# Token-wise projections, the residual's carry on another engine, q's rms inside the exponential, and a new order of weights in the last passes

## The chip, the cores and the metric

One core of a Trainium2 chip. The metric is the device time of one execution in microseconds (us); the median of three runs is given. Engines: PE (matrix products), ACT, DVE (vector) and POOL, each with an instruction stream of its own that runs in program order; SP issues the loads.

## The reference

Two layers run over 512 latent and 128 context tokens with 1024 features. Layer 0 mixes tokens by a Hyena long convolution, layer 1 by attention; each layer then has a gated ConvFFN with 2816 hidden features. Cut to what the change touches:

```
z = h @ w_qkv + b_qkv                    # 1024 -> 8 q heads, 2 k heads, 2 v heads of 128
q = z_q * rsqrt(mean(z_q^2) + eps) * q_gain ;  k likewise, with k_gain
q, k = rotate(q), rotate(k)              # rotary positions, latent tokens only
p = softmax(q @ k^T * 128**-0.5) ;  out = (p @ v) @ w_o + b_o
x = layer_norm(alpha * x + (1 + gate) * out) * ln_g + ln_b
h = x * (1 + scale) + shift              # what the next projection reads
```

Latent queries see 512 latent and 256 cached keys, context queries the 128 context keys.

## The kernel before

Everything is float32, and a product of float32 numbers is made of three matmuls over a high and a low half of both operands (`mm3`, L339 to L341): high by high, high by low, low by high. PE therefore reads every weight as a pair of tiles (`whl`): ACT casts the loaded piece to its high half (L334), and DVE or POOL subtracts to get the low half (L335). Loads land in `raw` (three buffers, issued by SP at L226); the pairs rotate through a ring of three, so a cast waits until PE has done with the pair three back.

The 640 tokens are five tiles of 128: `LAT3` = 0, 1, 2, `REST` = 3, 4 (4 is the context), `ALL5`. A projection whose result has tokens on the partitions is a `TokenPass`. `run` goes over the weight pieces j and for each over the tiles, all tiles adding up in PSUM at once; only the last `tail` pieces go tile by tile, and after each tile `done(i)` reads its sums. `hooks` are functions called at a piece's number, which puts their instructions at that place in each engine's stream. `prep` splits the weights, `ahead` pieces before they are used.

**Out-projections** (`out_passes`, `out_projection`): a pass over LAT3, then one over REST with the same weights (the ConvFFN's second half; its first half is an ALL5 pass). When REST starts, three groups of weights are still in the ring, and two groups (`Keep`) stand split in tiles of the old h. Other groups are loaded again. `begin` sets the order of the groups: the ring's oldest, the first kept, the ring's others, the other kept one, then the reloaded ones. After a tile's sums `last` runs on DVE: gate and residual (L634, L639), statistics (L528, L529), a reciprocal root by Newton steps (L511 to L520), then ACT normalises (L542). During REST the hooks `finish` call `make_h` for tiles 0, 1, 2: PE transposes x (L496) and ACT and DVE scale it into the next h. `at` says at which piece: 0, 1, 3 in the Hyena and attention projections, 1, 5, 10 in the ConvFFN's. Tiles 3 and 4 get theirs during the next projection.

**Attention** (`attention`): four passes make k, v (`ps[0]` LAT3, `ps[1]` REST) and q (`ps[2]`, `ps[3]`, four heads each, ALL5), without a tail: all five tiles end together. `biased` adds the bias (L1106), `squares` sums squares on ACT (L1126), `rms` makes the reciprocal roots, `normed` multiplies by them (L1141) and rotates (a product on POOL at L1147, two operations on DVE, L1151 and L1152). `kv_turn` and `q_turn` transpose on PE (L1157). The second half of q (`ps[3]`) is normed and turned inside the attention. There 32 units of work (8 heads by 4 tiles of latent queries) follow one another: scores, maximum (L1277), exponential (L1279), division by the sum on POOL (`normalise`, L1226), transposes (L1286), split, product with v. `carry` multiplies x by alpha times ln_g and adds ln_b's part, ten operations of 128x1024 (L663) over the five tiles, for the residual after the attention; it is on POOL, one operation every second unit from unit 12.

Of the kernel before, what the change touches and what calls it, by code (L numbers as in the profile page):

```python
# [202 lines left out]
class TokenPass:  # L203
# [89 lines left out]
class Build:  # L293
# [320 lines left out]
    def out_passes(self, acts, kt, w, h, tail=3, lag=2):  # L614
# [10 lines left out]
    def out_projection(self, passes, xs, gates, finish, hooks=None, final=None, early=None, mid=None, after=None):  # L625
# [25 lines left out]
        at = (0, 1, 3) if whole else (1, 5, 10)  # L651
# [396 lines left out]
    def qkv_pass(self, h, c, toks, before=None):  # L1048
# [6 lines left out]
        return self.tm_pass(act, KD, self.io["qkv"][c], 1, toks, self.nc.vector, before)  # L1055

    def attention(self, h, hstack, ap, oT, outs, pending, first, carry):
# [9 lines left out]
        st = ExitStack()  # L1067
        rp = self.pool(st, "rope")
# [6 lines left out]
        def prepare():  # L1075
# [7 lines left out]
            for t, j in ((g, 0), (gs, 1)):  # L1083
                nc.sync.dma_start(out=t.rearrange("p a d -> p (a d)"), in_=io["gains"][j:j + 1].broadcast_to([P, 2 * P]))
            for t, nm in enumerate(("k", "q")):
# [17 lines left out]
        def biased(c0):  # L1103
# [24 lines left out]
        def rms(c0, nh, toks, have=()):  # L1128
            n = nh * len(toks)
            for i in toks:  # L1130
                if i not in have:
                    squares(c0, nh, toks, i)
# [352 lines left out]
```

## Time and profile before

| | |
|---|---|
| median of 3 runs | 1657.54 us (1654.52 to 1657.75) |
| profiled execution | 1658.16 us, of which the span is 1656.4 us |
| PE busy | 95% of the span |
| DVE, ACT, POOL busy | 58%, 39%, 31% |
| mean granted TensorE clock | 0.983 |

The profile is of one execution. A row of the timeline gives the start in the span, the time, engine, line, operation and tiles, then in brackets how long the engine had waited and for what. PE works throughout except for the first tenth of the span and a few short stops, so what a change is worth is read at these stops, and at the clock that is granted after them.

### The profile page before, as it was taken

How to read it: one execution, taken by the hardware profiler on the slowest of the kernel's cores; microseconds unless marked ns; L12 is line 12 of the kernel's file. 1: busy time of each engine (PE TensorE's matmuls, PEld its weight loads, DVE VectorE, ACT ScalarE, POOL GpSimd, SP SyncE). 2: the span in 40 equal slices, each digit the busy share in tenths (PEclk: the TensorE clock that was granted, in tenths of full speed). 3: DMA queues.
4: the chain of work that ended last, by engine and by line, in shares of the span. 5: the costliest groups of instructions: out<-in, count | busy, mean ns of one | idle time of the engine just before them, and what ended most of it. 6: DMA issues, size and time to landing. Idle time of an engine off the chain costs nothing.

```text
span 1656.4 us, 23775 instructions
## 1 busy us (share of the span) xinstructions
PE 1580.9 (95%) x9545; PEld 1419.3 (86%) x9545; DVE 959.3 (58%) x1575; ACT 652.8 (39%) x1237; POOL 506.2 (31%) x330
## 2 busy tenths in 40 slices
PE   6799999999999999999999998699999999999996
PEld 3689999978999999998887777698999999997885
DVE  5637467677433443355577668777654365345586
ACT  3433223335433333343445337573543333334331
POOL 4533233400344445430001015720065455430000
PEclk9899999999999999999999999799999999999998
DMA  7776341342344444431234200402212122221231
GB/s 267 252 277 249 136 185 64 135 155 102 128 179 141 165 165 155 152 103 64 80 127 150 70 1 27 165 29 77 102 52 103 52 101 90 102 77 64 76 128 51
DMA packets 35445, 198.66 MB, mean 120 GB/s; under 512 B 3946, under 2 KB 5254, under 8 KB 15494
## 3 DMA queue, kind: packets, MB, share of 16 engines
q1 hardware_dynamic: 35334, 197.13, 33.5%
q8 instruction: 75, 1.23, 0.3%
q14 instruction: 36, 0.29, 0.1%
HBM read 188.91 MB, written 8.20 MB: 119 GB/s over the span
## 4 chain that ended last, share of the span: by engine, by line
PE 82%; DVE 8%; POOL 3%; issue 3%; ACT 3%; DMA 1%; SPq 0%; POOLq 0%; DVEq 0%; ACTq 0%
PE p L339 25%; PE p L341 25%; PE p L340 25%; PE p L398 2%; POOL x L663 1%; DMA raw<-in_w_mod 1%; PE p L496 1%; DVE whl L335 1%; DVE x L639 1%; PE p L1286 1%; DVE small L634 1%; DVE bnst L528 1%; POOL whl L335 1%; ACT act L1126 0%; DVE small L1151 0%
## 5 line engine op out<-in xcount | busy, mean ns | idle before, releaser
L335 POOL TENSOR_TENSOR whl<-raw,whl 128x1024 fp32r<-128x1024 f32 x104 | 255.4, 2460 | 351.1 <-ACT whl L334 291.9
L339 PE MATMUL p<-hhA,whl 128*128 128x384 f32 x880 | 301.4, 342 | 0.0
L341 PE MATMUL p<-hhA,whl 128*128 128x384 f32 x880 | 296.5, 337 | 0.5 <-POOL whl L335 0.5
L340 PE MATMUL p<-hlA,whl 128*128 128x384 f32 x880 | 296.5, 337 | 0.0
L334 ACT CAST whl<-raw 128x1024 fp32r<-128x1024 f32 x193 | 202.3, 1050 | 212.6 <-PE p L340 173.9
L340 PE MATMUL p<-hlB,whl 128*128 128x256 f32 x880 | 247.3, 281 | 0.0
L341 PE MATMUL p<-hhB,whl 128*128 128x256 f32 x880 | 246.9, 281 | 0.0
L339 PE MATMUL p<-hhB,whl 128*128 128x256 f32 x880 | 246.7, 280 | 0.0
L339 PEld LDWEIGHTS p<-hhA,whl 128*128 128x128 f32 x880 | 166.0, 189 | 17.7 <-issue 15.9
L593 ACT ACTIVATE zs<-p,fv 128x128 f32<-128x128 f32 (+1 forms) x264 | 105.0, 435 | 162.5 <-PE p L341 156.7
L341 PEld LDWEIGHTS p<-hhA,whl 128*128 128x128 f32 x880 | 165.8, 188 | 1.4 <-POOL whl L335 1.4
L340 PEld LDWEIGHTS p<-hlA,whl 128*128 128x128 f32 x880 | 165.9, 189 | 0.9 <-issue 0.8
L598 DVE SCALAR_TENSOR_TENSOR act<-zs,fv,act 128x642 f32<-128x642 f32 x44 | 45.5, 1034 | 209.0 <-POOL act L597 209.0
L339 PEld LDWEIGHTS p<-hhB,whl 128*128 128x128 f32 x880 | 166.2, 189 | 0.0
L340 PEld LDWEIGHTS p<-hlB,whl 128*128 128x128 f32 x880 | 165.8, 188 | 0.0
L341 PEld LDWEIGHTS p<-hhB,whl 128*128 128x128 f32 x880 | 165.7, 188 | 0.0
L340 PE MATMUL p<-whl,act 128*128 128x512 f32 x364 | 143.9, 395 | 0.0
L341 PE MATMUL p<-whl,act 128*128 128x512 f32 x364 | 142.1, 396 | 1.6 <-DVE act L335 1.6
L339 PE MATMUL p<-whl,act 128*128 128x512 f32 x364 | 143.3, 394 | 0.0
L335 DVE TENSOR_TENSOR whl<-raw,whl 128x1024 fp32r<-128x1024 f32 x89 | 108.8, 1223 | 47.9 <-ACT whl L334 45.7
L598 DVE SCALAR_TENSOR_TENSOR small<-zs,fv,small 128x642 f32<-128x642 f32 x44 | 41.2, 935 | 128.4 <-POOL small L597 128.4
L597 POOL TENSOR_SCALAR small<-zs,fv 128x642 f32<-128x642 f32 x44 | 46.6, 1059 | 208.0 <-ACT zs L593 208.0
(351 smaller groups left out, 3094.0 us busy)
## 6 DMA issues: line engine op xcount, KB each, us to landing
raw<-in_w_mod SPq DMA_DIRECT2D x48, 1024.0 KB, 5.2
raw<-in_ff_in SPq DMA_DIRECT2D x44, 1024.0 KB, 4.8
raw<-in_ff_out SPq DMA_DIRECT2D x26, 1024.0 KB, 5.0
raw<-in_hy_in SPq DMA_DIRECT2D x12, 1024.0 KB, 6.4
raw<-in_qkv SPq DMA_DIRECT2D x7, 1024.0 KB, 5.1
raw<-in_hy_out SPq DMA_DIRECT2D x6, 1024.0 KB, 7.1
raw<-in_at_o SPq DMA_DIRECT2D x6, 1024.0 KB, 5.0
Kd<-act SPq DMA_DIRECT2D x20, 256.0 KB, 2.9
```

What stands on the lines that cost most here:

```text
L334: self.nc.scalar.copy(out=hi, in_=full)
L335: (lo_eng or self.nc.vector).tensor_tensor(out=lo, in0=full, in1=hi.bitcast(F32), op=ALU.subtract)
L339: mm(out, lhsT=sh, rhs=mh, start=start, stop=False)
L340: mm(out, lhsT=sh, rhs=ml, start=False, stop=False)
L341: mm(out, lhsT=sl, rhs=mh, start=False, stop=stop)
L398: nc.tensor.matmul(ps[32 * j:32 * j + 32, :], lhsT=self.condT[:, k, :], rhs=raw[:, j * 512:(j + 1) * 512], start=(k == 0), stop=(k == KD - 1),
L496: nc.tensor.transpose(out=ps[:, kk * P:(kk + 1) * P], in_=x[:, k * P:(k + 1) * P], identity=self.ident)
L528: nc.vector.bn_stats(out=st[:, j, :], in_=x[:, j * 512:(j + 1) * 512])
L593: nc.scalar.activation(dst, src, AF.Identity, bias=bias)
L597: nc.gpsimd.tensor_scalar(out=t, in0=zs[:, 1:1 + WO], scalar1=w[1], scalar2=cb, op0=ALU.mult, op1=ALU.add)
L598: nc.vector.scalar_tensor_tensor(out=t, in0=zs[:, 0:WO], scalar=w[0], in1=t, op0=ALU.mult, op1=ALU.add)
L634: nc.vector.tensor_tensor(out=t, in0=p, in1=g[:, cs], op=ALU.mult)
```

## The change

**Out-projections.** The REST pass takes the ring's three groups first, then the reloaded ones, then the two kept. Its tail grows from 3 to 5 pieces of 8 in the Hyena and attention projections and from 4 to 8 (layer 0) or 10 (layer 1) of 22 in the ConvFFN. New hooks `t0`, `t1`, ... run ahead of each tile of the tail, and the pass that follows gets two of its pieces prepared before the tail. The places of `finish` become 2, `t0`, `t1` (Hyena), 1, 4, 9 (ConvFFN) and 0, 1, `t0` (attention).

**qkv passes.** All four get a tail of 4 pieces of 8. The squares follow each tile's bias at once, and in the q passes the norm of the tile before. Tables, cache loads, norms and turns of k move to other hooks. The second half of q is normed at the end of `ps[3]` and turned at units 1, 3, 5, 7, 9.

**q's rms in the exponential.** q is no longer multiplied by its reciprocal root (ten operations of L1141 go). The root times 128**-0.5 is a number per query: its negative multiplies the row's maximum, and it is the exponential's scale, a column instead of a constant.

**The carry** goes from POOL to DVE, from the attention to hooks of `ps[2]` and `ps[3]`, with row buffers of its own.

Cut to its core, the diff:

```diff
@@ TokenPass.begin
-        held = p.ring[:1] + (p.keep.groups[:1] if p.keep else []) + p.ring[1:] + (p.keep.groups[1:] if p.keep else [])
-        self.ws = {g: p.ws[g] for g in held}
-        gs = held + [g for g in range((self.kt + self.wk - 1) // self.wk) if g not in held]
+        kept = p.keep.groups if p.keep else []
+        self.ws = {g: p.ws[g] for g in p.ring + kept}
+        gs = p.ring + [g for g in range((self.kt + self.wk - 1) // self.wk) if g not in self.ws] + kept
@@ TokenPass.run
         self.prep(kt - 1)
+        if follow:
+            follow.prep(1)
...
-        for i in self.toks:
+        for t, i in enumerate(self.toks):
+            for f in hooks.get(f"t{t}", ()):
+                f()
             for j in range(kt - self.tail, kt):
                 product(j, i)
             done(i, [outs[i, n] for n in range(nn)])
@@ out_passes (end=8, for the ConvFFN of layer l: 8 + 2 * l)
-            return p + [self.tm_pass(act, kt, w, 2, REST, v, p[0], tail=3, ahead=2)]
+            return p + [self.tm_pass(act, kt, w, 2, REST, v, p[0], tail=5, ahead=2)]
...
-        return p + [self.tm_pass(act, kt, w[1], 1, REST, v, p[1], tail=4, ahead=4)]
+        return p + [self.tm_pass(act, kt, w[1], 1, REST, v, p[1], tail=end, ahead=4)]
@@ out_projection (Hyena: at=(2, "t0", "t1"), attention: at=(0, 1, "t0"))
-        at = (0, 1, 3) if whole else (1, 5, 10)
+        at = at or (1, 4, 9)
@@ qkv_pass
-        return self.tm_pass(act, KD, self.io["qkv"][c], 1, toks, self.nc.vector, before)
+        return self.tm_pass(act, KD, self.io["qkv"][c], 1, toks, self.nc.vector, before, tail=4)
@@ attention, biased (q_norm now passes None for the root)
                 zb[c0, i] = z
+                squares(c0, nh, toks, i)
+                if nh == 4 and i:
+                    q_norm(c0 // 512, i - 1)
@@ attention, rms
+                nc.vector.tensor_scalar_mul(ng, rs, -SCALE)
+                nc.vector.tensor_scalar_mul(ps, rs, SCALE)
@@ attention, normed
-            nc.vector.tensor_tensor(out=z, in0=z, in1=rs.broadcast_to([P, nh, P]), op=ALU.mult)
+            if rs is not None:
+                nc.vector.tensor_tensor(out=z, in0=z, in1=rs.broadcast_to([P, nh, P]), op=ALU.mult)
@@ attention, the passes
-        ps[0].run(biased(1024), plan((2, pending[0]), (3, prepare), (4, pending[1]), (6, caches)), ps[1])
-        ps[1].run(biased(1024), plan((0, rms, 1024, 2, LAT3), (0, kv_norm, 0), (2, kv_norm, 1), (3, kv_turn, 0), (4, kv_norm, 2),
-                                     (6, kv_turn, 1)), ps[2])
...
+        carry = self.carry(xs, self.dn, nc.vector, lambda s: rp.tile(s, F32, tag="row", name=self.uid("row"), bufs=2), True)
+        ps[0].run(biased(1024, 2, LAT3), plan((1, next, prep), (2, next, prep), (3, pending[0]), ("t0", pending[1]), ("t1", next, prep),
+                                              ("t2", caches)), ps[1])
+        ps[1].run(biased(1024, 2, REST), plan((0, rms, 1024, 2, LAT3), (0, kv_norm, 0), (1, kv_norm, 1), ("t0", kv_turn, 0),
+                                              ("t0", kv_norm, 2), ("t1", kv_turn, 1)), ps[2])
+        ps[2].run(biased(0, 4, ALL5), plan((0, rms, 1024, 2, REST), (0, kv_norm, 3), (1, kv_norm, 4), (1, kv_turn, 2), (2, next, carry),
+                                           (3, next, carry), (3, next, carry), ("t0", kv_turn, 3), ("t0", next, carry), ("t1", kv_turn, 4),
+                                           ("t1", next, carry)), ps[3])
+        ps[3].run(biased(512, 4, ALL5), plan((0, bias, 512), (0, q_norm, 0, 4), (0, rms, 0, 4, ALL5), *[(i, q_turn, 0, i) for i in range(4)],
+                                             *[(i, next, carry) for i in range(4)], ("t0", next, carry), ("t0", q_turn, 0, 4),
+                                             *[(f"t{u + 2}", first_scores, u) for u in range(2)]))
...
+        q_norm(1, 4)
@@ attention, scores
-                nc.vector.tensor_scalar_mul(mx, mx, -SCALE)
-                nc.scalar.activation(pr, s[:, :, 0:384], AF.Exp, bias=mx, scale=SCALE, accum_out=sm)
+                ng, sc = row_scales(u)
+                nc.vector.tensor_tensor(out=mx, in0=mx, in1=ng, op=ALU.mult)
+                nc.scalar.activation(pr, s[:, :, 0:384], AF.Exp, bias=mx, scale=sc, accum_out=sm)
...
-                if u >= 12 and u % 2 == 0:
-                    next(carry, None)
```

The tables below are the compiled order of instructions: line, operation, output<-inputs, shape. In the changed file lines stand 5 to 23 further down (L335 is L340, L496 is L501, L663 is L668, L1106 is L1114, L1141 is L1160, L1147 is L1166, L1157 is L1176).

The first place is PE at the start of the Hyena projection's REST pass (xyr is the split input, x_826 is tile 0's x). Before:

```order
L339 MATMUL p_433_3267<-whl_3503,hhA_3442 128x512
L340 MATMUL p_433_3267<-whl_3504,hhA_3442 128x512
L341 MATMUL p_433_3267<-whl_3503,hlA_3443 128x512
L496 MATMUL p_496_3649<-ident,x_826 128x128 x4
L496 MATMUL p_498_3661<-ident,x_826 128x128 x4
L339 MATMUL p_492_3645<-whl_3314,xyr_3476 128x512
L340 MATMUL p_492_3645<-whl_3315,xyr_3476 128x512
```
Now:

```order
L345 MATMUL p_494_3647<-whl_3343,xyr_3511 128x512
L346 MATMUL p_494_3647<-whl_3342,xyr_3511 128x512
L344 MATMUL p_495_3648<-whl_3342,xyr_3511 128x512
L345 MATMUL p_495_3648<-whl_3343,xyr_3511 128x512
L346 MATMUL p_495_3648<-whl_3342,xyr_3511 128x512
L501 MATMUL p_501_3683<-ident,x_826 128x128 x4
L501 MATMUL p_503_3695<-ident,x_826 128x128 x4
L344 MATMUL p_492_3645<-whl_3503,xyr_3511 128x512
```
The transposes of tile 0 stood ahead of the pass's first product; now 24 products of it (1985 to 2008 in PE's stream) go first.

The second place is the end of `ps[1]`. On PE before (hhB and hlB are h of REST, small_8355 and small_8357 are k of tiles 0 and 1):

```order
L341 MATMUL p_1063_8362<-whl_8316,hlB_6968 128x512
L339 MATMUL p_1062_8361<-whl_8316,hhB_6967 128x512
L340 MATMUL p_1062_8361<-whl_8317,hhB_6967 128x512
L341 MATMUL p_1062_8361<-whl_8316,hlB_6968 128x512
L1157 MATMUL p_1073_8420<-ident,small_8355 128x128 x2
L339 MATMUL p_1063_8362<-whl_8316,hhB_6967 128x512
L340 MATMUL p_1063_8362<-whl_8317,hhB_6967 128x512
L341 MATMUL p_1063_8362<-whl_8316,hlB_6968 128x512
L1157 MATMUL p_1078_8456<-ident,small_8357 128x128 x2
L339 MATMUL p_1062_8361<-whl_8446,hhB_6967 128x512
```
Now (small_8319 and small_8341 are k of tiles 0 and 1; hhA with p_1087 is `ps[2]`):

```order
L344 MATMUL p_1067_8372<-whl_8428,hhB_6967 128x512
L345 MATMUL p_1067_8372<-whl_8429,hhB_6967 128x512
L346 MATMUL p_1067_8372<-whl_8428,hlB_6968 128x512
L1176 MATMUL p_1079_8438<-ident,small_8319 128x128 x2
L1176 MATMUL p_1084_8468<-ident,small_8341 128x128 x2
L344 MATMUL p_1087_8490<-whl_8434,hhA_6965 128x512
L345 MATMUL p_1087_8490<-whl_8435,hhA_6965 128x512
```
The transposes stood in the middle of the pass's 48 products; now they are behind all of them and ahead of `ps[2]`.

On DVE at the same place, before:

```order
L335 TENSOR_TENSOR whl_8447<-raw_8444,whl_8446 128x1024
L518 TENSOR_TENSOR sd_1070_8376<-rq_1068_8374 128x6
L519 TENSOR_TENSOR sd_1070_8376<-sd_1070_8376,ve_1069_8375 128x6
L520 SCALAR_TENSOR_TENSOR rq_1068_8374<-sd_1070_8376,rq_1068_8374 128x6
L1141 TENSOR_TENSOR small_8355<-small_8355,rq_1068_8374 128x256
L1141 TENSOR_TENSOR small_8357<-small_8357,rq_1068_8374 128x256
L1141 TENSOR_TENSOR small_8359<-small_8359,rq_1068_8374 128x256
L1151 TENSOR_TENSOR small_8355<-small_8355,kta 128x256
L1151 TENSOR_TENSOR small_8357<-small_8357,kta 128x256
L1152 TENSOR_TENSOR small_8355<-small_8355,act_8391 128x256
L1152 TENSOR_TENSOR small_8357<-small_8357,act_8410 128x256
L1151 TENSOR_TENSOR small_8359<-small_8359,kta 128x256
```
Now:

```order
L340 TENSOR_TENSOR whl_8533<-raw_8432,whl_8532 128x1024
L523 TENSOR_TENSOR sd_1070_8376<-rq_1068_8374 128x6
L1114 TENSOR_TENSOR small_8485<-p_1067_8372,qkvb_8212 128x512
L524 TENSOR_TENSOR sd_1070_8376<-sd_1070_8376,ve_1069_8375 128x6
L340 TENSOR_TENSOR vl<-small_8462,vh 128x256
L525 SCALAR_TENSOR_TENSOR rq_1068_8374<-sd_1070_8376,rq_1068_8374 128x6
L340 TENSOR_TENSOR whl_8582<-raw_8579,whl_8581 128x1024
L1160 TENSOR_TENSOR small_8319<-small_8319,rq_1068_8374 128x256
L1160 TENSOR_TENSOR small_8341<-small_8341,rq_1068_8374 128x256
L1160 TENSOR_TENSOR small_8366<-small_8366,rq_1068_8374 128x256
L1170 TENSOR_TENSOR small_8319<-small_8319,kta 128x256
L1170 TENSOR_TENSOR small_8341<-small_8341,kta 128x256
```
k's norm stood ahead of the bias additions of `ps[1]` (L1106); now both bias additions (L1114), that of tile 4 among them, and the split of the pair whl_8581, whl_8582 stand ahead of the norm (L1160, L1170).

The third place is POOL inside the attention, before:

```order
L663 TENSOR_TENSOR x_828<-x_828,raw_9545 128x1024
L663 TENSOR_TENSOR x_829<-x_829,raw_9545 128x1024
L1226 TENSOR_SCALAR raw_9329<-raw_9329,sm_9384 128x2x384
L663 TENSOR_TENSOR x_3261<-x_3261,raw_9545 128x1024
L663 TENSOR_TENSOR x_826<-x_826,raw_9985 128x1024
L663 TENSOR_TENSOR x_827<-x_827,raw_9985 128x1024
L663 TENSOR_TENSOR x_828<-x_828,raw_9985 128x1024
L663 TENSOR_TENSOR x_829<-x_829,raw_9985 128x1024
L1226 TENSOR_SCALAR pr_9435<-pr_9435,sm_9437 128x768
L1147 TENSOR_TENSOR qkvb_9538<-small_8967,qtb 128x512
```
Now:

```order
L1249 TENSOR_SCALAR raw_8922<-raw_8922,sm_1166_8967 128x2x384
L1166 TENSOR_TENSOR qkvb_9001<-small_8953,qtb 128x512
L1166 TENSOR_TENSOR qkvb_9024<-small_8994,qtb 128x512
L1249 TENSOR_SCALAR raw_9047<-raw_9047,sm_9049 128x2x384
L1249 TENSOR_SCALAR raw_9047<-raw_9047,sm_9077 128x2x384
L1249 TENSOR_SCALAR raw_9112<-raw_9112,sm_9114 128x2x384
L1249 TENSOR_SCALAR raw_9112<-raw_9112,sm_9162 128x2x384
```
The operations on x are gone from between the divisions by the sum. On DVE, whose hooks for them stand in `ps[2]` and `ps[3]`, the compiled order has all ten between the transposed tile 3 in `ps[0]` and the first turn of k behind `ps[1]`.

## Rows read from the trace of the kernel before

**Rows 1.** The page, part 1: busy time, share of the span, instructions.
```profile
PE 1580.9 (95%) x9545; PEld 1419.3 (86%) x9545; DVE 959.3 (58%) x1575; ACT 652.8 (39%) x1237; POOL 506.2 (31%) x330
```

**Rows 2.** Timeline of PE: start, us, engine, line, operation, tiles, [wait before it].
```profile
368.80 0.40 PE L339 MATMUL p<-whl,hhA 128*128 128x512 f32 x1
...
369.27 0.40 PE L341 MATMUL p<-whl,hlA 128*128 128x512 f32 x1
374.32 1.82 PE L496 MATMUL p<-ident,x 128*128 128x128 f32 x8 [4.65 <-ACT x L542]
...
927.88 0.44 PE L1157 MATMUL p<-ident,small 128*128 128x128 f32 x2 [1.53 <-DVE small L1152]
...
975.33 1.11 PE L1157 MATMUL p<-ident,small 128*128 128x128 f32 x4 [3.19 <-DVE small L1152]
```

**Rows 3.** Busy time by stretch, as headed; PEclk is the granted clock.
```profile
core 0: us, PE busy (x) PEld busy (x) DVE busy (x) ACT busy (x) POOL busy (x), PEclk, DMA share, GB/s
374.50:377.90 3.40, 3.40 (x13) 3.02 (x13) 3.40 (x16) 1.87 (x4) 0.00 (x0) 0.50 0.02 5
975.30:978.70 3.40, 3.37 (x12) 3.00 (x13) 3.40 (x5) 1.17 (x2) 1.48 (x1) 0.50 0.02 5
1038.60:1043.50 4.90, 4.90 (x22) 4.80 (x23) 3.81 (x8) 1.36 (x3) 4.90 (x3) 0.50 0.00 0
1055.00:1060.60 5.60, 5.56 (x26) 5.56 (x27) 4.34 (x5) 2.61 (x6) 4.88 (x3) 0.50 0.72 227
```

**Rows 4.** PE's waits from 890 to 1120: us in total, times, longest.
```profile
PE p L1286 <- POOL pr L1226: 9.7, 4, 8.1
PE p L1157 <- DVE small L1152: 6.3, 3, 3.2
PE p L339 <- DVE pl L335: 4.8, 2, 4.5
PE p L496 <- ACT x L542: 2.0, 2, 1.2
PE s L339 <- ACT raw L1279: 1.4, 1, 1.4
```

**Rows 5.** Timeline of POOL from 1025 to 1060: carry operations in one piece.
```profile
1042.04 12.06 POOL L663 TENSOR_TENSOR x<-x,raw 128x1024 f32<-128x1024 f32 x5
```

**Rows 6.** Timeline of ACT: make_h's predecessor at 373, a weight cast at 931.
```profile
373.03 1.24 ACT L542 ACTIVATE x<-x,nm,rs 128x1024 f32<-128x1024 f32 x1 [6.62 <-DVE nm L539]
...
931.85 1.05 ACT L334 CAST whl<-raw 128x1024 fp32r<-128x1024 f32 x1 [1.70 <-PE p L340]
```

**Rows 7.** Timeline of DVE around k's norm, 922 to 935.
```profile
924.11 1.64 DVE L1141 TENSOR_TENSOR small<-small,rq 128x256 f32<-128x256 f32 x3
...
931.69 1.28 DVE L1106 TENSOR_TENSOR small<-p,qkvb 128x512 f32<-128x512 f32 x2
932.93 1.23 DVE L335 TENSOR_TENSOR whl<-raw,whl 128x1024 fp32r<-128x1024 f32 x1
```

**Rows 8.** By line: number, ns min/median/max, first and last start.
```profile
L663 DVE TENSOR_TENSOR x<-x,raw x20: 1212/1220/3428, 604.1 to 1390.4; 128x1024 f32<-128x1024 f32 x20
...
L1151 DVE TENSOR_TENSOR small<-small,qta x8: 678/1218/2850, 971.2 to 1056.3; 128x512 f32<-128x512 f32 x8
...
L1147 POOL TENSOR_TENSOR qkvb<-small,qtb x4: 1259/1274/1292, 1019.2 to 1055.0; 128x512 f32<-128x512 f32 x4
```

**Rows 9.** The end: last matmul on PE, then DVE.
```profile
1642.77 0.40 PE L341 MATMUL p<-whl,hid_r 128*128 128x512 f32 x1
...
1644.47 0.68 DVE L634 TENSOR_TENSOR small<-p,bc 128x512 f32<-128x512 f32 x1
...
1648.47 1.41 DVE L1445 SCALAR_TENSOR_TENSOR x<-x,rs,lnb 128x512 f32<-128x512 f32 x2
```

**Rows 10.** The page, part 6: KB, us from issue to landing; then SP's timeline.
```profile
raw<-in_hy_out SPq DMA_DIRECT2D x6, 1024.0 KB, 7.1
...
356.99 0.33 SPq L226 DMA_DIRECT2D raw<-in_hy_out  x1
```

More of the change, by code (lines that the diff above doesn't have):

```diff
@@ L612, in act_split, with out_passes @@
         return act, lambda k: full.rest(self, k)
-    def out_passes(self, acts, kt, w, h, tail=3, lag=2):
+    def out_passes(self, acts, kt, w, h, tail=3, lag=2, end=8):
         v = self.nc.vector
@@ L1054, in act, with attention @@
             return [r]
-        return self.tm_pass(act, KD, self.io["qkv"][c], 1, toks, self.nc.vector, before)
-    def attention(self, h, hstack, ap, oT, outs, pending, first, carry):
+        return self.tm_pass(act, KD, self.io["qkv"][c], 1, toks, self.nc.vector, before, tail=4)
+    def attention(self, h, hstack, ap, oT, outs, pending, first, xs):
         nc, io, tc = self.nc, self.io, self.tc
@@ L1126, in squares, with rms @@
                 nc.scalar.activation(sq[:, j], zb[c0, i][:, j], AF.Square, accum_out=sums[c0][:, t * nh + j:t * nh + j + 1])
-        def rms(c0, nh, toks, have=()):
+        def rms(c0, nh, toks):
             n = nh * len(toks)
-            for i in toks:
-                if i not in have:
-                    squares(c0, nh, toks, i)
             ss = sums.pop(c0)
@@ L1136, in rms @@
             self.rstd(ss, rs.rearrange("p h o -> p (h o)"), n, 1)
+            if nh == 4:
+                ng = rp2.tile([P, n], F32, name=f"ng{c0}")
+                ps = rp2.tile([P, n], F32, name=f"ps{c0}")
+                rs = rs.rearrange("p h o -> p (h o)")
+                nc.vector.tensor_scalar_mul(ng, rs, -SCALE)
+                nc.vector.tensor_scalar_mul(ps, rs, SCALE)
+                for t, i in enumerate(toks):
+                    scales[c0, i] = ng[:, t * nh:(t + 1) * nh], ps[:, t * nh:(t + 1) * nh]
+                return
             for t, i in enumerate(toks):
@@ L1229, in attention @@
         ps = [first, self.qkv_pass(h, 2, REST, first)] + [self.qkv_pass(h, c, ALL5) for c in (0, 1)]
-        ps[0].run(biased(1024), plan((2, pending[0]), (3, prepare), (4, pending[1]), (6, caches)), ps[1])
-        ps[1].run(biased(1024), plan((0, rms, 1024, 2, LAT3), (0, kv_norm, 0), (2, kv_norm, 1), (3, kv_turn, 0), (4, kv_norm, 2),
-                                     (6, kv_turn, 1)), ps[2])
-        ps[2].run(biased(0), plan((0, rms, 1024, 2, REST), (0, kv_norm, 3), (1, kv_norm, 4), (2, kv_turn, 2), (4, kv_turn, 3),
-                                  (5, kv_turn, 4)), ps[3])
-        ps[3].run(biased(512), plan((0, bias, 512), (0, rms, 0, 4, ALL5), *[(i, q_norm, 0, i) for i in range(5)],
-                                    *[(i + 2, q_turn, 0, i) for i in range(5)], *[(6, first_scores, u) for u in range(2)]))
+        prep = prepare()
+        carry = self.carry(xs, self.dn, nc.vector, lambda s: rp.tile(s, F32, tag="row", name=self.uid("row"), bufs=2), True)
[9 more added lines that the diff above has]
+                                             *[(f"t{u + 2}", first_scores, u) for u in range(2)]))
+        for _ in carry:
+            pass
+        q_norm(1, 4)
         hstack.close()
@@ L1404, in run @@
         pending = self.out_projection(passes, xs, lambda: env["gates"], finish, {3: [hook]}, None,
-                                      *[lambda i=i: self.ffn_first(0, i) for i in range(3)])
+                                      *[lambda i=i: self.ffn_first(0, i) for i in range(3)], (2, "t0", "t1"))
         bst.close()
@@ L1414, in run @@
             act = self.act_split(hid)
-            passes = self.out_passes(act, KF, io["ff_out"][l], lambda: env["h"])
+            passes = self.out_passes(act, KF, io["ff_out"][l], lambda: env["h"], end=8 + 2 * l)
             fill = self.mods_units(1, (0, 1, 2)) if l == 0 else iter(())
```

29 lines of the change are left out of this document (17 added, 12 removed).

## The prediction

> **What bounds the kernel now.** I read the page's busy times first: PE is busy for 95% of the span [rows 1], and the change leaves the number of matmuls as it is. So time can come only from PE's stops, from the slower clock behind them, and from what runs after the last matmul. The timeline of PE gives three stops on which the change acts, of 4.65, 1.53 and 3.19 us [rows 2]; the reader is to see the tile that PE waited for. The table by stretch shows what follows a stop: PE is full, yet the granted clock is 0.50, the lower of its two levels (1.2 and 2.4 GHz), for 3.4 us after the stops of 4.65 and 3.19, for 4.9 and 5.6 us after two in the attention [rows 3]. Half of such a stretch is lost, 1.7 to 2.8 us. The waits of PE from 890 to 1120 [rows 4] name the causes there. The largest is 8.1 us for one division on POOL, and POOL's timeline shows why: five carry operations, 12.06 us in one piece, stood ahead of it [rows 5].
>
> **The change part by part.** The sum is made against the profiled execution, 1658.16 us, 0.6 above the median of the runs.
>
> *Hyena's REST pass.* Tile 0's transposes wait for its normalisation on ACT, which ends at 373.03 + 1.24 = 374.27 [rows 6], and start at 374.32 [rows 2]; PE had been idle since 369.67. Now 24 products of the pass stand ahead. Products there start 0.235 us apart (368.80 to 369.27 for two [rows 2]), so they take 5.6 us, and the stop of 4.65 is covered if the normalisation ends no later than before. It may: the projection's last steps run on DVE as they did, and if they slip by half of the stop, 1.3 is left. I take it as covered but for 0.1, and with it go 1.7 of half clock: **-6.3** (bounds -3.3, the 1.3 and its clock left, and -6.4). Tiles 1 and 2 are later by as much as their transposes are.
>
> *Weights in a new order.* Casts and subtractions are as many as before. The reloaded groups are now wanted after the ring's three and not after five. The last load of the Hyena projection is issued at 356.99 and a load takes 7.1 us [rows 10], so it has landed at 364, over 5 us before the pass starts at 369.67: nothing. The same order holds in the other three REST passes; its risk is a rival below.
>
> *ConvFFN of layer 0.* With more of the tail, tiles 3 and 4 end further apart, and their transposes in `ps[0]` come after the normalisation instead of before it. The two waits for L542, 2.0 us [rows 4], go: **-2.0** (0 to -2.0).
>
> *k's first turn.* This is a new wait. The transposes were among the products of `ps[1]`, where they waited 1.53 us [rows 2]. They are now behind the pass's last product, and on DVE k's norm is behind the bias addition of tile 4 and behind the split of a pair whose slot the same last product frees. So nothing of it can begin before PE stops. The cast takes 1.05 on ACT [rows 6], the subtraction 1.23, the bias addition (0.64, half of 1.28) lies beside the cast [rows 7]. From the norm's first product to the transposes were 927.88 - 924.11 = 3.77 us [rows 2, 7]. Together 6.1 us of stop. One or two carry operations, 1.22 each [rows 8], may still be unfinished when PE stops: up to 8.5. I take 7.2 and, between the 1.7 after a stop of 3.19 and the 2.8 after one of 8.1, 2.5 for the clock; the old 1.53 goes: **+8.2** (bounds -1.5, if the scheduler's order costs nothing, and +9.8). Behind the waiting transposes on PE is all of `ps[2]`; nothing on DVE waits for them.
>
> *The carry in `ps[0]` and `ps[1]`.* Ten operations of 1.22 [rows 8] are 12.2 us on DVE in about 30 us where it had gaps. PE sees them where a subtraction for a pair comes late: **+0.3** (0 to +2).
>
> *q's first turn.* It waited 3.19 for a norm that started only after all of q was summed. The multiplication by the root is gone and the rotation runs tile by tile in the tail, ahead of the next pass. The stop goes, and 1.7 of half clock [rows 2, 3]: **-4.9** (0 to -4.9).
>
> *The attention.* Waits on POOL's divisions (9.7), on the split of the probabilities (4.8), on the exponential (1.4) and 1.6 of the turns (6.3 less 1.53 and 3.19) are 17.5 us [rows 4]; the two stretches of 4.9 and 5.6 us at half clock add 5.25 [rows 3]. All of it stood where POOL ran the carry or where the second half of q was normed between units, and both are gone. What is new is at its start: the last rotations of q's second half. Each needs a POOL product of 1.27 and then one on DVE of 0.68 to 2.85 [rows 8], they share one scratch tile, and the maximum of unit 2 stands among them on DVE, its exponential behind them. One round takes 1.95 to 4.1. PE had no slack there, it already waited 1.4 at this place. So 1.4 at least, 1.4 + 2 x 4.1 = 9.6 at most; I take 1.4 + 4.1 = 5.5, one round at its longest or two at their shortest, and 1.7 of clock; and later once more 1.4. New 8.6, old 22.75: **-14.2** (bounds -21.4 and -8.3, with 2.8 of clock).
> The exponential's scale as a column has no row of its own; L542 on ACT has a column for the scale too and takes 1.24 for 1024 elements [rows 6], so I cost it at nothing.
>
> *The end.* The last matmul ends at 1643.17, but tile 4's first step on DVE comes at 1644.47, 1.3 late, and tile 3's last one (1.41 at 1648.47) stands between its steps [rows 9]. With a tail of 10 pieces tile 3 is done long before: **-2.6** (0 to -2.7).
>
> Sum: -6.3 - 2.0 + 8.2 + 0.3 - 4.9 - 14.2 - 2.6 = -21.5, which gives 1636.7; against the median 1636. The forecast is **1636 us**.
>
> **The rivals.** *The new waits are small (1621 us).* If the norm of k is done when PE gets there, 8.2 goes; if unit 2's maximum is no later than before, so do the 7.2 above the 1.4. 1636 - 15.4 = 1621. For it: before, DVE did k's norm in 3.77 us inside a running pass [rows 7]. Against: the order of DVE, where the norm is behind a cast that PE's last product releases.
>
> *DVE becomes the bound (1649 us).* The carry on DVE has 1.22 as its median but 3.43 as its longest, and DVE's rotation has 0.68 and 2.85 [rows 8]: both read two inputs. If the ten carry operations and the rotations of the attention's start are all long ones, DVE is up to 10 x 2.2 = 22 us later between `ps[0]` and the attention; PE sees what is behind it at k's turn and at unit 2's maximum, about half, and the time is 1636 + 13 = 1649. It decides at whether POOL's products run at the same moments. Against it: POOL has only k's and q's rotation there, a few microseconds in all, since the weights of these passes are split by DVE. The Trainium skill, "SBUF — State Buffer", in the section that says who interferes with whom, has DVE and GpSimd share a pair of ports as an exclusive lock, which a DVE operation with two SBUF inputs takes against a GpSimd operation that reads SBUF, the later one being blocked to the end of the earlier one; the page speaks against moving the carry beside POOL's products, and the rotation's longest, 2.85 [rows 8], agrees with it, since it lay beside an operation of the carry on POOL. By it the carry costs this rival's time only where the two streams meet.
>
> *Slower: late weights (1676 us).* The two kept groups gave the reloads time at the head of each of four REST passes. If a reload now lands after the ring's three groups are used up, PE waits up to a load, 7.1 us [rows 10], and runs 2.8 us longer at half clock: 4 x 9.9 = 40 us, 1636 + 40 = 1676. It decides where a load is issued less than 7.1 us and a cast and subtraction (2.3) before its place. Against it: the one place with rows has 12 us from issue to the pass's start.
>
> *It does not do what it says.* The divisions on POOL could be late without the carry too, as 32 of them are still there. Then some 8 of the 14.2 stay: 1644, inside the range.
>
> **How the numbers follow.** Forecast (with 1628 to 1645 as its own range) 0.52; small waits 0.20; DVE as the bound, the unmoved divisions with it, 0.22; late weights 0.06. The second and third case spread to both sides of their time by the bounds of the single costs, so the range goes 2 or 3 us past each, 1619 to 1652; it leaves out some 0.06 of either and all of the last, 0.18. What a measurement here can tell from no change is 0.2%, 3.3 us. A third-case result high enough to be within it has 0.03, late weights in one or two passes only another 0.01. So faster 0.91, same 0.04, slower 0.05.
>
> **What would show it.** In the profile after: no wait for L542 (L547 there) of over 1 us at the Hyena's REST pass, and no half clock behind it; one new wait of 6 to 8.5 us for k's rotation right after `ps[1]`, with about 5 us at 0.50 behind it; no wait of over 1 us at q's turn; no wait for POOL of over 2 us in the attention, one of about 5 near its start; the last matmul followed by less than 8 us on DVE. I am wrong if REST passes wait for weights, if the attention's waits are the same in sum, or if the carry's operations on DVE have a median far above 1.2.

## The result, and the profile after

The changed kernel takes 1632.8 us (median of 4 runs, 1632.59 to 1633.5) against 1657.32 before (4 runs): ratio 0.9859, 95% interval 0.9845 to 0.9874, 24.5 us less. The profiled execution's span is 1631.1 us, with a mean granted clock of 0.988.

The page's busy times, which answer to [rows 1]:

```profile
PE 1574.6 (97%) x9545; PEld 1413.9 (87%) x9545; DVE 961.2 (59%) x1579; ACT 656.5 (40%) x1237; POOL 479.0 (29%) x320
```

PE's busy time fell by only 6.3 us while the span fell by 25.3. So most of what went was time in which PE stood, the end of the span included, and the rest half clock, at which the same products are busy for longer.

PE's waits from 350 on (us in total, times, longest), which answer to [rows 4]:

```profile
PE p L1176 <- DVE small L1171: 7.3, 1, 7.3
PE s L344 <- ACT raw L1312: 4.3, 1, 4.3
PE p L346 <- DVE act L340: 1.6, 2, 0.8
PE p L1319 <- POOL pr L1249: 1.3, 2, 1.0
PE p L1319 <- ACT oT L1203: 1.2, 1, 1.2
PE s L344 <- ACT pr L1312: 1.2, 1, 1.2
```

The waits of [rows 4] on L542 (L547 now) and on POOL's long division are gone; the longest for a division is 1.0. Two large ones are new: 7.3 us for k's rotation and 4.3 us for the exponential of unit 2. PE's timeline has the first right behind the last product of `ps[1]`:

```profile
920.01 0.40 PE L346 MATMUL p<-whl,hlB 128*128 128x512 f32 x1
927.72 1.11 PE L1176 MATMUL p<-ident,small 128*128 128x128 f32 x4 [7.32 <-DVE small L1171]
```

Busy time by stretch, as in [rows 3], shows what the two stops cost beyond themselves. The clock falls to 0.50 while PE stands and stays there for 5.1 and 3.2 us of full work, 2.5 and 1.6 us lost:

```profile
core 0: us, PE busy (x) PEld busy (x) DVE busy (x) ACT busy (x) POOL busy (x), PEclk, DMA share, GB/s
922.60:927.70 5.10, 0.00 (x0) 0.00 (x0) 4.48 (x10) 1.43 (x9) 2.62 (x3) 0.50 0.83 284
927.70:932.80 5.10, 5.08 (x14) 4.16 (x15) 4.93 (x15) 0.75 (x2) 0.00 (x0) 0.50 0.00 0
1001.30:1004.50 3.20, 3.19 (x12) 3.09 (x13) 3.05 (x6) 1.64 (x4) 0.91 (x1) 0.50 0.61 218
```

After the last matmul ([rows 9] before) DVE goes on at once with tile 4, and tile 3's last step (1619.06) is already through. First PE, then DVE:

```profile
1620.18 0.39 PE L346 MATMUL p<-hhB,hid_r 128*128 128x512 f32 x1
```

```profile
1619.06 1.41 DVE L1475 SCALAR_TENSOR_TENSOR x<-x,rs,lnb 128x512 f32<-128x512 f32 x2
1620.60 0.69 DVE L639 TENSOR_TENSOR small<-p,bc 128x512 f32<-128x512 f32 x1
...
1625.98 1.41 DVE L1475 SCALAR_TENSOR_TENSOR x<-x,rs,lnb 128x512 f32<-128x512 f32 x2
```

The table gives the length of each stretch in PE's timeline, in us, from one stage's first product to the next's; the first begins where Hyena's LAT3 pass ends, the last runs from the last matmul to the span's end. All runs of this study are in it. It leaves out what lies ahead of LAT3's end, which differed by up to 6 us between profiled executions (1.0 between before and after), in stages that no run changes. Each row is of one profiled execution.

| run | Hyena REST | ConvFFN 0 | k, v passes | q passes | attention | out-proj., ConvFFN 1 | end | sum |
|---|---|---|---|---|---|---|---|---|
| before | 31.4 | 496.5 | 34.5 | 65.9 | 121.8 | 523.6 | 13.2 | 1286.9 |
| after | 25.1 | 496.4 | 38.5 | 63.0 | 105.8 | 523.3 | 10.5 | 1262.6 |
| control | 25.1 | 496.4 | 38.8 | 63.0 | 105.7 | 523.3 | 10.5 | 1262.7 |
| turns_late | 25.1 | 496.4 | 30.1 | 63.8 | 106.3 | 523.3 | 10.5 | 1255.4 |
| scratch | 25.1 | 496.4 | 38.3 | 63.3 | 102.6 | 523.3 | 10.5 | 1259.6 |
| carry_pool | 25.1 | 496.4 | 32.0 | 61.0 | 124.0 | 522.9 | 10.4 | 1271.8 |
| rest_old | 31.3 | 496.1 | 41.3 | 62.2 | 106.9 | 523.7 | 13.2 | 1274.7 |
| keep_old | 27.7 | 497.9 | 42.7 | 62.4 | 107.0 | 524.5 | 12.5 | 1274.7 |
| tails_old | 27.2 | 496.6 | 40.8 | 63.1 | 105.8 | 523.6 | 13.2 | 1270.3 |
| carry_raw | 25.1 | 496.4 | 32.6 | 62.5 | 107.1 | 523.3 | 10.5 | 1257.4 |
| raw_scratch | 25.1 | 496.4 | 33.6 | 62.3 | 102.1 | 523.3 | 10.5 | 1253.2 |
| q_old | 25.1 | 496.4 | 38.4 | 66.6 | 102.6 | 523.3 | 10.4 | 1262.8 |
| best1 | 25.1 | 496.4 | 29.8 | 61.6 | 102.9 | 523.2 | 10.5 | 1249.4 |
| best1_q_old | 25.1 | 496.4 | 29.9 | 65.0 | 103.3 | 523.3 | 10.4 | 1253.3 |

Between before and after: -6.3 in Hyena's REST pass, +4.0 in the k, v passes, -2.9 in the q passes, -16.0 in the attention, -2.7 at the end.

### The profile page after: what moved, and what is told of

Same layout as the page of the kernel before. It is cut to its first block, busy times and chain, and to the rows that moved or that the text cites. A ratio compares the mean times of both kernels' runs of the same rounds, so it can differ in the third digit from the quotient of the medians.

```text
span 1631.1 us, 23761 instructions
## 1 busy us (share of the span) xinstructions
PE 1574.6 (97%) x9545; PEld 1413.9 (87%) x9545; DVE 961.2 (59%) x1579; ACT 656.5 (40%) x1237; POOL 479.0 (29%) x320
## 4 chain that ended last, share of the span: by engine, by line
PE 85%; DVE 6%; issue 4%; POOL 2%; ACT 2%; DMA 1%; SPq 0%; POOLq 0%; DVEq 0%; ACTq 0%
PE p L344 26%; PE p L345 26%; PE p L346 26%; PE p L403 2%; PE p L1319 1%; DMA raw<-in_w_mod 1%; PE s L344 1%; PE s L346 1%; PE s L345 1%; PE p L501 1%; POOL whl L340 1%; DVE whl L340 1%; DMA row<-dn 0%; DVE x L668 0%; ACT whl L339 0%
## 5 line engine op out<-in xcount | busy, mean ns | idle before, releaser
L340 POOL TENSOR_TENSOR whl<-raw,whl 128x1024 fp32r<-128x1024 f32 x104 | 255.6, 2461 | 347.1 <-ACT whl L339 291.1
L340 DVE TENSOR_TENSOR whl<-raw,whl 128x1024 fp32r<-128x1024 f32 x89 | 108.6, 1222 | 35.9 <-ACT whl L339 33.3
```

What stands on the lines that cost most here:

```text
L340: (lo_eng or self.nc.vector).tensor_tensor(out=lo, in0=full, in1=hi.bitcast(F32), op=ALU.subtract)
```

## The experiments

All are edits of the changed kernel, with ratios to the kernel before on the same chip. The control, the changed kernel again, gave 0.9862 [0.9848, 0.9877].

> The changed kernel itself, unaltered, so that the runs beside it have it on the same chip. All theories: its ratio to the kernel before is again 0.986, the stop at k's turn again 7.3 us.

It held: 1632.96 us, and a stop of 7.3 us.

**turns_late: k's turns inside the first q pass.**

```diff
-    ("t0", kv_turn, 0), ("t0", kv_norm, 2), ("t1", kv_turn, 1)), ps[2])
+    ("t0", kv_norm, 2)), ps[2])
...
-    (1, kv_norm, 4), (1, kv_turn, 2), (2, next, carry),
+    (1, kv_norm, 4), (2, kv_turn, 0), (3, kv_turn, 1), (3, kv_turn, 2), (2, next, carry),
```

> The changed kernel, with k's turns of tiles 0, 1, 2 moved behind the second and third piece of the first q pass (30 and 45 products) instead of right behind the last k, v pass. Theory (the stop of 7.3 us is only a matter of where the transposes stand: k's norm cannot start on DVE before the pass ends): the stop falls to under 0.6 us, the 5 us at half clock behind it (2.5 lost) go too, so 1632.8 - 9.5 = about 1623. Rival (DVE is simply too loaded there, with the carry among its work): the stop comes back at the later transposes or at a weight split of the first q pass, and no more than 3 us are won, 1630 or more.

Measured 1625.37, ratio 0.9823 [0.9807, 0.9839]. The stretches fall by 7.2 us. The theory's direction holds, and the rival's 1630 did not come; the theory asked for 9.5, and 2.0 us of waits stayed at the later turns.

**carry_pool: the carry back on POOL.**

```diff
-    carry = self.carry(xs, self.dn, nc.vector, lambda s: rp.tile(s, F32, tag="row", name=self.uid("row"), bufs=2), True)
+    carry = self.carry(xs, self.dn, nc.gpsimd, self.raw, True)
...
+    if u >= 12 and u % 2 == 0:
+        next(carry, None)
```

> The changed kernel with the carry back on POOL, one operation every second unit from unit 12 of the attention, as before the change; all else as in the change. Theory (the carry on POOL made the long waits of the attention): waits for POOL's divisions and for DVE's splits of about 8 to 12 us in sum come back, with 2 to 5 us at half clock, so 1632.8 + 10 to 14 = about 1645; k's turn waits about 1.2 us less, 6.1 instead of 7.3. Rival (the norms of q's second half between the units made them, and these stay gone): less than 4 us are lost, 1636 or less.

Measured 1640.59, ratio 0.9918 [0.9902, 0.9934]. The attention is 18.3 us longer than in the changed kernel. PE is busy for 106.0 of its 124.0 us, against 97.0 of 105.8, so 9.3 us of this are stops and 8.9 half clock: the carry's place made most of its long waits. The one wait of 8.1 for a division did not come back; the longest is 2.0. But the k, v and q passes are 8.6 shorter, so that the time is under the 1645 expected. PE's waits:

```profile
PE s L344 <- ACT raw L1308: 8.0, 2, 4.4
PE p L1315 <- POOL pr L1249: 4.5, 5, 2.0
PE p L344 <- DVE pl L340: 1.9, 1, 1.9
...
PE p L1176 <- DVE small L1171: 1.6, 1, 1.6
```

k's turn waits 1.6, not the 6.1 I expected. DVE's timeline in this run shows why: the multiplication by k's root (L1160) starts at 912.10, straight behind the last Newton step. The steps from L517 on had begun at 909.06 and took 3.0 us, with one weight split among them:

```profile
911.90 0.17 DVE L525 SCALAR_TENSOR_TENSOR rq<-sd,rq 128x6 f32<-128x6 f32 x1
912.10 1.64 DVE L1160 TENSOR_TENSOR small<-small,rq 128x256 f32<-128x256 f32 x3
```

In the changed kernel the same steps (L517 to L525) begin at 913.61, behind five carry operations (L668). Among them and ahead of the multiplication stand three more carry operations, four weight splits of 1.21 us and two bias additions (L1114). They take 10.2 us, and the multiplication comes at 923.84, behind the pass's end at 920.4:

```profile
913.61 0.16 DVE L517 TENSOR_SCALAR rq<-ve 128x6 int32<-128x6 int32 x1
913.68 1.22 DVE L668 TENSOR_TENSOR x<-x,row 128x1024 f32<-128x1024 f32 x1
914.82 0.15 DVE L523 TENSOR_TENSOR sd<-rq 128x6 f32<-128x6 f32 x1
914.90 1.21 DVE L340 TENSOR_TENSOR whl<-raw,whl 128x1024 fp32r<-128x1024 f32 x1
916.03 0.15 DVE L524 TENSOR_TENSOR sd<-sd,ve 128x6 f32<-128x6 f32 x1
916.11 1.21 DVE L668 TENSOR_TENSOR x<-x,row 128x1024 f32<-128x1024 f32 x1
917.24 0.15 DVE L525 SCALAR_TENSOR_TENSOR rq<-sd,rq 128x6 f32<-128x6 f32 x1
...
919.20 1.21 DVE L668 TENSOR_TENSOR x<-x,row 128x1024 f32<-128x1024 f32 x1
...
920.41 1.21 DVE L340 TENSOR_TENSOR whl<-raw,whl 128x1024 fp32r<-128x1024 f32 x1
...
921.62 0.68 DVE L1114 TENSOR_TENSOR small<-p,qkvb 128x512 f32<-128x512 f32 x1
...
922.71 1.21 DVE L340 TENSOR_TENSOR whl<-raw,whl 128x1024 fp32r<-128x1024 f32 x1
923.84 1.08 DVE L1160 TENSOR_TENSOR small<-small,rq 128x256 f32<-128x256 f32 x3
925.54 1.79 DVE L1170 TENSOR_TENSOR small<-small,kta 128x256 f32<-128x256 f32 x2 [0.62 <-POOL act L1166]
```

So the stop at k's turn seems to be the carry's doing.

**carry_raw: the carry on DVE, later.** This tests that directly.

```diff
-    carry = self.carry(xs, self.dn, nc.vector, lambda s: rp.tile(s, F32, tag="row", name=self.uid("row"), bufs=2), True)
+    carry = self.carry(xs, self.dn, nc.vector, self.raw, True)
```

> The changed kernel with the carry still on DVE, but its rows loaded into the three raw buffers of the weights and not into buffers of their own; a row's load then waits for its turn in that ring, and the second row's five operations come on DVE behind k's norm (10 us later than now). Theory, formed from the run with the carry on POOL, where k's turn waited 1.6 and not 7.3 us: the carry's operations, one between each two steps of k's reciprocal root, push k's norm behind the pass's end; the order of DVE I had put the stop down to is their doing. So the stop falls from 7.3 to under 3 us, with its 2.5 at half clock: 5 to 8 us faster than the control. Rival (the transposes' place behind the pass is enough for the stop): 6 us of it stay, under 2 us faster. A price to look for in both: splits of weights in the q passes that wait for a load, up to 2 us.

Measured 1625.11, ratio 0.9817 [0.9802, 0.9832]. The k, v passes take 32.6 instead of 38.8 and the stop is 2.0; the attention is 1.3 longer than the control's. For the stop the theory holds, and the rival falls. Half clock came all the same: PE runs at 0.50 from 917.4 to 920.8, 1.7 us lost, so most of the 2.5 was not won. turns_late took the stop away with the carry in its old place. So the stop needs both, the transposes right behind the pass and the carry ahead of the norm.

**scratch: a third buffer for q's scratch.**

```diff
-    qb[c0] = rp.tile([P, 512], F32, tag="qkvb", name=f"qkvb{c0}", bufs=2)
+    qb[c0] = rp.tile([P, 512], F32, tag="qkvb", name=f"qkvb{c0}", bufs=3)
...
-    t = rp.tile([P, 512], F32, tag="qkvb", name=self.uid("qkvb"), bufs=2)
+    t = rp.tile([P, 512], F32, tag="qkvb", name=self.uid("qkvb"), bufs=3)
```

> The changed kernel with three instead of two buffers for the bias rows and q's scratch tiles, so that the second half of q has two scratch tiles for its squares and POOL products. Theory (at the start of the attention the maximum of unit 2 is late because POOL's products wait for the one scratch tile): the waits of 4.3 and 1.4 us there shrink by 4 to 6 us and with them most of the 1.6 us lost to half clock, so 1626 to 1629. Rival (the sum of DVE's and ACT's work behind the last q pass is what takes the time, whatever the buffers): under 1 us is won, 1632 or more.

Measured 1630.76, ratio 0.9857 [0.9842, 0.9871], not told apart from the control by the runs. The trace has the attention 3.1 us shorter than the control's: the wait of 4.3 is gone, one of 2.2 for a split is new:

```profile
PE p L1319 <- DVE pl L340: 2.2, 1, 2.2
```

The buffer is one cause and DVE's work behind it the next, so the answer lies between the two theories.

**raw_scratch: both edits.**

> The two edits together: the carry's rows in the raw buffers, and three buffers for q's bias rows and scratch tiles. If the two act at different places, as the theory has it, their gains add up: what the run with the rows in raw buffers wins, and 3 us more (the third buffer took 3.0 us out of the stretch from the end of the last q pass to the attention's out-projection). Rival (they share a cause, DVE's load): clearly less than the sum.

Measured 1623.15, ratio 0.9803 [0.9787, 0.982]. By the stretches 9.6 us won against 5.3 and 3.2 for the edits alone: they add up.

**q_old: q's handling as before.**

```diff
+    nc.vector.tensor_tensor(out=z, in0=z, in1=rs.broadcast_to([P, nh, P]), op=ALU.mult)
...
-    nc.scalar.activation(pr, s[:, :, 0:384], AF.Exp, bias=mx, scale=sc, accum_out=sm)
+    nc.scalar.activation(pr, s[:, :, 0:384], AF.Exp, bias=mx, scale=SCALE, accum_out=sm)
...
+    *[(2 * i + 6, q_norm, 1, i) for i in range(5)], *[(2 * i + 7, q_turn, 1, i) for i in range(5)]
```

> The changed kernel with q's handling as before: q multiplied by its root, first half normed and turned in the second q pass, second half normed and turned between the units of the attention, constant scale in the exponential; the carry stays on DVE. Theory (q's part is worth the stop at q's first turn, 3.19 us and 1.7 at half clock, and inside the attention little either way, since the carry made the long waits there): 4 to 8 us slower than the control, the attention within 3 us of it. Rival (the norms between the units were half of the attention's waits): 12 us or more slower.

Measured 1634.54, ratio 0.9869 [0.9854, 0.9883]. Neither theory held. The stop at q's turn is back (the 10.5 here are 7.3 at k's turn and 3.2 at q's), and the q passes are 3.6 us longer; but the attention is 3.1 shorter. Its start no longer holds the second half's rotations, and the wait for the exponential there is 0.9, not 4.3. In the changed kernel q's part wins nothing that can be told: 0.1 us by the stretches, 1.6 by the medians. The attention also confirms the carry's price: with q's old handling it takes 102.6 us here and 121.8 in the kernel before, with the carry on POOL, 19.2 more, and with the new handling it was 18.3.

```profile
PE p L1164 <- DVE small L1159: 10.5, 2, 7.3
```

**rest_old: the out-projections' part undone.** The old lines of the diff for `begin`, the tails and `at`, of which the first:

```diff
-    gs = p.ring + [g for g in range((self.kt + self.wk - 1) // self.wk) if g not in self.ws] + kept
+    gs = held + [g for g in range((self.kt + self.wk - 1) // self.wk) if g not in held]
```

> The changed kernel with the part on the out-projections undone: order of the weight groups, tails of the REST passes (3, 4, 4) and places of finish as before; the qkv passes and the attention as in the change. Theory (that part is worth the Hyena's stop, 6.2 us with its half clock, and the end, 2.7; the order of the weights by itself nothing): 1632.8 + 8.9 = about 1642, and up to 2.4 more if the waits for tiles 3 and 4 in the first k, v pass come back too, 1644. Rival (the new order of weights takes away waits in every REST pass): 1648 or more.

Measured 1643.93, ratio 0.9934 [0.9917, 0.9952], 12 us slower by the stretches: Hyena's pass +6.2, the k, v passes +2.8, the end +2.7. The theory's upper end.

**keep_old: the order of the weights alone.** The old lines of `begin` only, as in the diff just above.

> The changed kernel with the weight groups of the REST passes in the old order (kept groups early, reloaded last), tails and places of finish as in the change. Theory (the gains of that part come from where the transposes and the tails stand; the order of the weights only moves which products come when, and loads are early in both): the same as the changed kernel within 0.2%, 1630 to 1636, every stretch between the passes' ends within 0.5 us. Rival (the reloads need the new order, or the kept groups' tiles are written by the next h too late in the new one): a stretch of a REST pass changes by 2 us or more.

Measured 1644.57, ratio 0.9931 [0.9918, 0.9945]. My theory fell: with the new tails in the old order all 12 us are lost. From its waits:

```profile
PE p L1176 <- DVE small L1171: 8.1, 1, 8.1
...
PE p L501 <- ACT x L547: 2.8, 2, 2.1
PE p L344 <- ACT hhA L339: 2.5, 1, 2.5
```

The compiled order of PE shows the reason. In the changed kernel the last ConvFFN's tail is 18 products with ring weights and 12 with kept ones for tile 3, then the same for tile 4. A tail of 10 pieces is five groups, and the ring holds three. With the kept groups early the tail is all ring groups; a fourth can only be split when tile 4 too has used the first, so tile 4's products are drawn in between tile 3's (18 of tile 3, 11 of tile 4, 1, 4, 11, 15), and the tiles end together again. DVE takes up tile 4's sums 4.1 us after tile 3's, where in the changed kernel it was 6.9 (1613.68 and 1620.60):

```profile
1627.02 0.69 DVE L639 TENSOR_TENSOR small<-p,bc 128x512 f32<-128x512 f32 x1 [1.52 <-PE p L346]
...
1631.09 0.68 DVE L639 TENSOR_TENSOR small<-p,bc 128x512 f32<-128x512 f32 x1
```

**tails_old: the old tails in the new order.**

```diff
-    REST, v, p[0], tail=5, ahead=2
+    REST, v, p[0], tail=3, ahead=2
...
-    REST, v, p[1], tail=end, ahead=4
+    REST, v, p[1], tail=4, ahead=4
```

> The changed kernel with the REST passes' tails as before (3, 4, 4 pieces), the new order of the weight groups and the new places of finish kept. With the old order and the new tails 12 us were lost, as much as with all of the out-projections' part undone. Theory (a tail of more pieces than the ring's three groups hold needs the kept groups at its end, so order and tail are worth something only together; the order alone only helps the Hyena's stop): the Hyena pass stays at 25.1 us, the end goes back to about 13.2 (2.7 lost), the waits for tiles 3 and 4 in the first k, v pass come back (2 to 3): 4 to 6.5 us slower than the changed kernel, a ratio to before of 0.9886 to 0.990. Rival (the order of the weights by itself made the gain): under 2 us slower.

Measured 1641.69, ratio 0.9917 [0.99, 0.9933]. By the stretches 7.7 us slower than the changed kernel, more than the 4 to 6.5 expected: the end is back at 13.2, Hyena's pass does not stay at 25.1 but loses 2.1, because the first product of the next stage waits for h, and the stop at k's turn is 9.6 us. I put the 2.3 us by which it grew down to the late tiles 3 and 4, which no run tested alone:

```profile
PE p L1176 <- DVE small L1171: 9.6, 1, 9.6
...
PE p L344 <- ACT hhA L339: 2.1, 1, 2.1
```

Of the 12.1 us that rest_old lost, the new tails in the old order win nothing back, and the new order with the old tails (and the new places of `finish`) 4.4. The rest needs both.

**best1: what the runs add up to.** raw_scratch, with k's turns of tiles 0, 1, 2 at pieces 1, 2, 3 of the first q pass:

```diff
-    ("t0", kv_turn, 0), ("t0", kv_norm, 2), ("t1", kv_turn, 1)), ps[2])
+    ("t0", kv_norm, 2)), ps[2])
...
+    (1, kv_turn, 0), (2, kv_turn, 1), (3, kv_turn, 2), (2, next, carry),
```

> The run with the carry's rows in the raw buffers and three scratch buffers, and k's turns of tiles 0, 1, 2 moved behind the first, second and third piece of the first q pass. There k's norm ended 2.9 us after the pass; 15 products take 3.5 us. Theory: the stop goes with its half clock (about 1.2 lost), 3 to 4.5 us faster than that run, 1619 to 1620. Rival (DVE is then late elsewhere in the q pass): under 1 us.

Measured 1618.87 (5 runs), ratio 0.9775 [0.9762, 0.9788], 14 us below the changed kernel. The stop at k's turn is gone from the waits; the largest left from the Hyena's REST pass on is

```profile
PE p L1318 <- DVE pl L340: 2.2, 1, 2.2
PE p L346 <- DVE act L340: 1.6, 2, 0.8
```

**best1_q_old: the same with q's old handling.**

> The fastest kernel so far (rows of the carry in the raw buffers, three scratch buffers, k's turns inside the first q pass) with q's handling as before the change: multiplied by its root, second half normed between the units, constant scale. In the changed kernel this cost nothing in sum, 3.6 us lost at q's first turn and 3.1 won at the attention's start, where q's scratch tiles were short. Theory (with three scratch buffers the start of the attention is no longer late, so what q's new handling wins at the turn is left): 2.5 to 4.5 us slower than the fastest, ratio to before 0.979 to 0.9805. Rival (q's handling is worth nothing whatever the buffers): within 1 us of the fastest.

Measured 1622.56, ratio 0.9805 [0.979, 0.9819], 3.9 us longer than best1 by the stretches. With the third scratch buffer there, q's new handling is worth what was expected of it.

## Why the prediction was right, and where its steps were not

Forecast 1636, measured 1632.8: right by the sum, and by most of its terms.

- **Hyena's REST pass:** -6.3 forecast, -6.3 measured. The 24 products cover the normalisation.
- **Tiles 3 and 4, and k's first turn:** -2.0 and +8.2 and 0.3, together +6.5; 2.5 of the 8.2 lie in the q passes, so +4.0 for the k, v passes. Measured +4.0, with a stop of 7.3 where I took 7.2. The order of DVE was read rightly, but the size was right by luck, since the step "*k's first turn*" put 6.1 us down to where the transposes and the weight split stand and gave the carry one or two unfinished operations. None of the ten ran in the stop: eight were done before it, and the last two, at 928.33 and 930.53, come behind k's rotation, where I had read all ten ahead of the turn. Nor did DVE stand for the cast that I counted. From PE's last product on it worked through two weight splits, the split of v, a bias addition and the last Newton steps, 3.4 us, and from the norm to the transposes it took 3.9. From the first carry operation to the norm DVE was busy for 25.82 of 25.84 us, so what stood there moved the norm. carry_pool showed that without the carry the stop is 1.6, not 6.1, and carry_raw that with five of its operations ahead of the norm and five behind it is 2.0. So the step "*The carry in `ps[0]` and `ps[1]`*: +0.3" is what failed: its price in the k, v and q passes is 8.6 us, most of which the sum had under k's first turn.
- **q's first turn:** -4.9 forecast. The q passes took 2.9 less with 2.5 of half clock from k's stop in them, so -5.4.
- **The attention:** -14.2 forecast, -16.0 measured, by a smaller start: 4.3 and 1.2 with 1.6 of clock instead of 8.6. The mechanism was right; the bound of -8.3 does not come out of its terms, which give -9.0 (22.75 less 9.6, 2.8 and 1.4). At the start the maximum of unit 2 (997.32 on DVE) stands behind a rotation, and its exponential's factor (999.99) behind the next:

```profile
994.94 1.74 DVE L1170 TENSOR_TENSOR small<-small,qta 128x512 f32<-128x512 f32 x1 [2.19 <-POOL qkvb L1166]
996.71 0.69 DVE L1171 TENSOR_TENSOR small<-small,qkvb 128x512 f32<-128x512 f32 x1
997.32 0.95 DVE L1309 TENSOR_REDUCE mx<-s 128x1 f32<-128x768 f32 x1
...
999.39 0.68 DVE L1171 TENSOR_TENSOR small<-small,qkvb 128x512 f32<-128x512 f32 x1
999.99 0.15 DVE L1311 TENSOR_TENSOR mx<-mx,ng 128x1 f32<-128x1 f32 x1
```

- **The end:** -2.6 forecast, -2.7 measured.
- **"*Weights in a new order*: nothing"** was wrong. I looked at loads and casts and not at what a tail may hold; keep_old lost 12 us, and its order of PE shows a tail of five groups in a ring of three. The sum did not suffer, since I had the long tails' gains in other terms.
- **q's rms:** the exponential with a column as its scale takes 0.996 us, with a constant it took 0.903; it is not "nothing", but ACT, busy for 40% of the span, has time for 30 times 0.093. By line, 20 of the 30, ns min/median/max, before and after:

```profile
L1279 ACT ACTIVATE pr<-s,mx x20: 897/903/935, 1041.5 to 1113.3; 128x768 f32<-128x768 f32 x20
```

```profile
L1312 ACT ACTIVATE pr<-s,mx,ps x20: 992/996/1053, 1031.2 to 1090.9; 128x768 f32<-128x768 f32 x20
```

The Trainium skill, "ScalarE: Activation LUTs", section "What ACT_TABLE_LOAD costs", gives about 93 ns for each operand that is a column and not a constant; the two rows agree.

Of the rivals, small new waits (1621) is what best1 makes of the change. DVE as the bound was right in the place it named, k's turn, where DVE had no gap left, and wrong in the cost: the carry's operations have a median of 1.21 us and one of them was long. (Its 13 us do not come out of its terms either; half of 22 is 11.) Late weights did not occur: PE's longest wait for a weight pair from 350 on is 0.4 us. And the divisions on POOL were late by the carry in the main: PE's waits for them, 9.7 us before, are 1.3 in the changed kernel and 4.5 in carry_pool. In q_old, with the carry off POOL and the norms between the units, they are 3.3.

## What to carry to other kernels

Moving long work off a crowded engine pays in full only where the new engine has no chain of short dependent steps in the same place: ten operations of 1.2 us won 18.3 us on POOL's side and cost 8.6 where eight of them stood ahead of and among the Newton steps of a small norm, and putting half of them later won 5 of that back. A buffer that decides how early something can start is also a handle on the compiled order, as the row buffers were here. And a long token-wise tail keeps its tiles apart only if all its weights are resident at once: count the groups that the ring and the kept tiles hold before choosing it.

## What the runs showed of the hardware that I had not expected

A carry operation on DVE took 2.32 us once and 1.21 to 1.22 in the nine others. POOL's product (first fence) began 0.05 us ahead of it and ended at 899.26, 1.24 us after the carry operation (second fence) began; 1.24 and 1.08, a little under one alone, are the 2.32:

```profile
897.97 1.29 POOL L1095 TENSOR_TENSOR qta<-act,gains 128x512 f32<-128x512 f32 x1
```

```profile
898.02 2.32 DVE L668 TENSOR_TENSOR x<-x,row 128x1024 f32<-128x1024 f32 x1 [0.70 <-DMA row<-dn]
```

carry_raw has another, where POOL's product ends at 926.68; 0.69 from the start of the carry operation to there and 1.08 are its 1.77. First POOL, then DVE:

```profile
925.88 0.80 POOL L1166 TENSOR_TENSOR act<-small,ktb 128x256 f32<-128x256 f32 x1 [9.63 <-DVE small L1160]
```

```profile
925.99 1.77 DVE L668 TENSOR_TENSOR x<-x,raw 128x1024 f32<-128x1024 f32 x1
```

The Trainium skill, "SBUF — State Buffer", section "Who interferes with whom", says that a DVE instruction with two SBUF inputs contends with a GpSimd (POOL) instruction that reads SBUF, that the ports they share are an exclusive lock, and that issue order decides who is blocked. Both cases agree.

In the changed kernel it happened to one carry operation of ten, the only one beside a product on POOL. DVE was busy for 25.82 of the 25.84 us from there to k's norm, so up to 1.1 us of the stop of 7.3 may be this. The rotation at 994.94 (above) is a third case, right ahead of unit 2's maximum: it took 1.74 instead of 0.68, beside the second of POOL's two products here, which ends at 996.13.

```profile
993.61 2.52 POOL L1166 TENSOR_TENSOR qkvb<-small,qtb 128x512 f32<-128x512 f32 x2 [0.36 <-ACT qkvb L1137]
```

So by the two durations about 1 us of the late maximum may be this; no run removes either alone.
